# Mixer tiles loaded into copy pages, a column sum's adding transfer in two halves and one gain held back, in a one-core encoder kernel

## The chip, the core and the metric

The kernel runs on one core of a Trainium2 chip. A core has TensorE (PE, the matrix engine), VectorE (DVE), ScalarE (ACT), GpSimd (POOL) and SyncE (SP), each with its own queue of instructions that it works off in order. SP issues most transfers (DMAs); POOL issues those that add to what lies at their destination. Sixteen DMA engines move the data. The metric is the time of one execution on the device in microseconds (us), as the median of three runs.

## What is computed

The reference is one layer of an encoder trunk on x of 1024 positions by 1024 channels, in float32:

```
proj = rmsnorm(x) @ w_in                    # 1024 x 8192, cut into glu_in, q, v, z_f, z_b, og, g_a, g_b
a    = silu(layernorm(dwconv31(glu(glu_in)))) @ conv_pw_w
o    = scan_forward(q, v, z_f) + scan_backward(q, v, z_b)      # 8 heads of 128, gated linear recurrence
bmix = (o * rsqrt(mean(o*o) + eps) * norm_w * silu(og)) @ hgrn_o_w
x    = x + (sigmoid(g_a) * a + sigmoid(g_b) * bmix) @ w_out
gate, val = split(rmsnorm(x) @ ffn_w_up)    # 2 x 2816 columns
x    = x + (silu(dwconv3(gate)) * val) @ ffn_w_down
out  = rmsnorm(x) * final_norm_w
```

## The kernel before

**Layout and products.** Activations stand transposed, 128 channels on the partitions and a half of 512 positions along them, in tiles of 128 x 512. Each float32 operand is split into a high and a low part (`split`, line 124: ACT casts the high part, DVE subtracts it from the source for the low part), and `mm3` (lines 148 to 150) makes a product of three matmuls: high by high, high by low, low by high. Split activations live in 32 pages `hx`, weights in four pages `wp` and three `wq`; raw weights come into two pages `wr`, other tiles into four pages `tm` (`tmp`, filled by `load`, line 117) and three pages `ev`.

**Pairs.** `pair_job` computes two column tiles of a projection at once with seven products in place of eight, from sums of the four weight quadrants. `rows` is the first tile's weights, `col` holds the column sums in a page `sw`: line 374 loads the first halves of both tiles into `col` and line 375 the second, then the whole second tile is added onto it by one transfer (`add`, line 301, issued by POOL; 512 KB). `sums` then makes row sums in place with two more adding transfers: `rows[:, :nk]` takes `col[:, nk:]`, and `rows[:, nk:]` takes `rows[:, :nk]`. They may begin when the split of `rows` into products 1 and 2 has read it. Products run in the order 1, 2, 6, 7, 5, 4, 3; 6 and 3 use the row sums, 7 and 5 the column sums. This form serves 13 of 19 pairs of the input projection (the other six add on DVE) and 19 of 22 pairs of the FFN (the other three load sums stored earlier).

**The scan.** While dense products run, 16 items (8 heads by 2 halves) go through the scan. `scan_base` and `scan_levels` use eight pages `A` of the pool `hp` for interleaved copies (`woven`, line 1177); the last matmuls that read them are on line 1196. `scan_states` transposes the keys, copies them to `kT` on ACT (line 1326) and copies the backward states to `Sb` (lines 1351 and 1353). `outputs` then sweeps `Sb` on DVE (line 1431), multiplies on PE (line 1374), takes means of squares, scales on ACT (line 1393), transposes, multiplies by gain and gate on DVE (line 1402) and stores the mixer tile in `d_bm` (line 1406). Head 7 is split at once instead.

**The seam.** After the last head, `bm_loads(half)` loads the seven stored tiles of a half through `load` into `tm` pages and splits them into `hx`, first half 0, later half 1. Around it run the pointwise convolution, whose results `gated_a` multiplies by a gate from `d_ga` and stores in `d_a` (lines 1104 to 1106), then the product with `hgrn_o_w`, whose results `merge` (lines 1511 to 1513) multiplies by a gate from `d_gb` and adds to `d_a`. `weight_sums` loads FFN weights (line 1544) beside it.

**The end.** The last four FFN rows are added in three parts: half 0, then two quarters of half 1, for each of eight column tiles. Per tile `final_evac` adds on DVE (line 1889), `turn_out` transposes back (line 1900), squares and sums on ACT (line 1902) and multiplies by the final gain on DVE (line 1915); after the eighth tile come the reduction, the power on POOL (line 1912), the scaling (lines 1936 and 1938) and the store (line 1940).

**What sets the order.** PE's order is that of the program. The order on the other engines, and on SP's queue, is chosen when the kernel is built, by a planner that goes by priority in program order and by estimated times; `pin` (`keep_in_program_order`) fixes instructions among themselves, and `tc.issue_after(i)` puts all instructions of a block that are on `i`'s engine behind `i`.

Of the kernel before, what the change touches and what calls it, by code (L numbers as in the profile page):

```python
# [15 lines left out]
ALU = mybir.AluOpType  # L16
AX = mybir.AxisListType

P = 128
# [18 lines left out]
def view(t, off, dims):  # L38

    return bass.AP(  # L40
        tensor=t.tensor,
        offset=t.offset + off,
        ap=[list(t.ap[0])] + [list(d) for d in dims],
    )
# [3 lines left out]
def tile_hybrid_encoder(  # L48
# [22 lines left out]
    nc = tc.nc  # L71
    PSUM = bass.MemoryType.PSUM
    V, A, G, T = nc.vector, nc.scalar, nc.gpsimd, nc.tensor

    S, D = x.shape[1], x.shape[2]
    ND = D // P
# [6 lines left out]
    NH = D // DK  # L83
# [19 lines left out]
    def page(pool, tag, bufs, dt=F32):  # L103
        return pool.tile([P, H], dt, tag=tag, name=nm(tag), bufs=bufs)
# [7 lines left out]
    def hx():  # L112
        return page(mp, "hx", 32, F32R)

    def load(src):
        t = tmp()
        nc.sync.dma_start(t, src)
        return t


    pin = tc.keep_in_program_order

    def split(hi, lo, src, eng, late=False):
        parts = A.copy(hi, src), eng.tensor_tensor(lo, src, hi.bitcast(F32), op=ALU.subtract)  # L124
        if late:
            for i in parts:
                pin(i)
        return hi, lo
# [153 lines left out]
    def pair_job(src0, src1, nk, acts, wpool, pool, evac, su=4, first=False, late=False, now=False, direct=False, columns=1, take=None, stored=None):  # L282
# [7 lines left out]
        def steps(w):  # L290
# [4 lines left out]
            def add(o, a):  # L295
                if first:
                    V.tensor_tensor(o, o, a, op=ALU.add)
                elif direct:
                    pin(V.tensor_tensor(o, o, a, op=ALU.add))
                else:  # L300
                    G.dma_start(o, a, accum_op=ALU.add)

            if take is not None:
# [11 lines left out]
                if stored is None:  # L315
# [3 lines left out]
                    col, sums, a22 = raw(), rows, other[:, nk:]  # L319
# [23 lines left out]
            def column_page():  # L343
                return wpool.tile([P, 2 * nk, P], F32, tag="sw", name=nm("sw"), bufs=columns)
# [26 lines left out]
                return  # L371

            col = column_page()
            nc.sync.dma_start(col[:, :nk], src0[:, :nk])
            nc.sync.dma_start(col[:, nk:], src1[:, :nk])
            if first:
                other = column_page()
                nc.sync.dma_start(other, src1)
                add(col, other)
            elif not direct:  # L380
                add(col, src1)
            def sums():
                add(rows[:, :nk], col[:, nk:])
                add(rows[:, nk:], rows[:, :nk])
# [757 lines left out]
    def tt(o, a, b, op=ALU.mult):  # L1142
        return V.tensor_tensor(o, a, b, op=op)  # L1143

    last_keys = []

    kscale = cp.tile([P, 2 * NH], F32, name="kscale")
    V.tensor_scalar(kscale, lbw[:, 3, :], DK**-0.5, None, op0=ALU.mult)
# [168 lines left out]
    def scan_states(i, kG, v, Tt, Sf, Sb):  # L1317

        half = i % 2
        kTs = []  # L1320
        for d in range(2):
            b = bank("mm" if d else "tr")
            for c in range(4):
                T.transpose(b[:, c * P : (c + 1) * P], kG[:, d, c * P : (c + 1) * P], ident)
            kT = page(hp, "kT", 2)
            A.copy(kT, b)
            kTs.append(kT)
        yield
        for d in range(2):
            u = bank("mm" if d else "sc")  # L1330
            for c in range(4):
                sl = slice(c * P, (c + 1) * P)
                T.matmul(u[:, sl], kTs[d][:, sl], v[:, c, :], start=True, stop=True)
            u4 = c4(u)
            if d == 0:
                for c in range(4 if half == 0 else 3):
                    nx = Sf[half][:, c + 1, :] if c < 3 else Sf[1][:, 0, :]
                    if half == 0 and c == 0:
                        V.tensor_copy(nx, u4[:, 0, :])
                    else:  # L1340
                        V.scalar_tensor_tensor(
                            nx,
                            Sf[half][:, c, :],
                            Tt[:, half, 0, c : c + 1],
                            u4[:, c, :],
                            op0=ALU.mult,
                            op1=ALU.add,
                        )
            else:

                A.copy(Sb[half][:, 0:3, :], u4[:, 1:4, :])
                if half == 1:
                    A.copy(Sb[0][:, 3, :], u4[:, 0, :])
        yield

    def scan_outputs(h, kept, Sf, Sb):


        ons, gates = [], []
        ss = cp.tile([P, 2, 4], F32, name=nm("oss"), tag="oss", bufs=2)  # L1360
        rs = cp.tile([P, 2, 4], F32, name=nm("ors"), tag="ors", bufs=2)
        for half in range(2):
            S_t, v, qF = kept[half]
            o = bank("ob")
            for c in range(4):
                sl = slice(c * P, (c + 1) * P)
                g = half * 4 + c
                terms = [(S_t[:, c, :], v[:, c, :])]
                if g > 0:
                    terms.append((qF[:, 1, sl], Sf[half][:, c, :]))  # L1370
                if g < 7:
                    terms.append((qF[:, 0, sl], Sb[half][:, c, :]))
                for n, (l, r) in enumerate(terms):
                    T.matmul(o[:, sl], l, r, start=(n == 0), stop=(n == len(terms) - 1))
            on = tmp()
            A.copy(on, o)
            for c in range(4):
                junk = hp.tile([P, DK], F32, tag="jk", name=nm("jk"), bufs=1)
                A.activation(  # L1379
                    junk, on[:, c * P : (c + 1) * P], AF.Square, accum_out=ss[:, half, c : c + 1]  # L1380
                )
            ons.append(on)
            gates.append(page(hp, "og", 2))
            nc.sync.dma_start(gates[half], d_og[h][half])
            if half == 0:
                yield
        rstd_small(rs, ss, DK)
        yield
        yield
        for half in range(2):  # L1390
            for c in range(4):
                sl = slice(c * P, (c + 1) * P)
                A.activation(
                    ons[half][:, sl], ons[half][:, sl], AF.Copy, scale=rs[:, half, c : c + 1]
                )
            yield
        for half in range(2):
            b = bank("tr")
            for c in range(4):
                T.transpose(b[:, c * P : (c + 1) * P], ons[half][:, c * P : (c + 1) * P], ident)  # L1400
            bt = ev()
            V.scalar_tensor_tensor(bt, b, vec("hn", h), gates[half], op0=ALU.mult, op1=ALU.mult)
            if h == NH - 1:
                bm[h][half] = split(hx(), hx(), bt, V)
            else:
                nc.sync.dma_start(d_bm[h][half], bt)
            yield
# [35 lines left out]

    def bm_loads(half):
        for h in range(NH - 1):
            bm[h][half] = split(hx(), hx(), load(d_bm[h][half]), V)

    NI = 2 * NH
    cur = Base(scan_inputs(0))
# [433 lines left out]

    PARTS = [(0, range(4)), (1, range(2)), (1, range(2, 4))]
    y_tags = itertools.cycle(["tr", "sc"])

    def final_evac(i, half, chunks, acc):
        t = xr[i][half][:, chunks[0] * P : (chunks[-1] + 1) * P]
        V.tensor_tensor(t, acc, t, op=ALU.add)
        later(8 - len(chunks), lambda: turn_out(i, half, chunks))  # L1890

    def turn_out(i, half, chunks):

        t, n = xr[i][half], len(chunks)
        if i == 0 and chunks[0] == 0:
            out_y.append(fy.tile([P, 4, D], F32, tag="y", name=nm("y"), bufs=2))
        ss, y = out_ss[half], out_y[half]
        b = bank(next(y_tags))[:, : n * P]
        for m, c in enumerate(chunks):
            T.transpose(b[:, m * P : (m + 1) * P], t[:, c * P : (c + 1) * P], ident)  # L1900
        for m, c in enumerate(chunks):
            A.activation(
                out_junk[c % 2], b[:, m * P : (m + 1) * P], AF.Square, accum_out=ss[:, i, c : c + 1]
            )
        those = slice(chunks[0], chunks[-1] + 1)
        if i == ND - 1:
            rs = cp.tile([P, 4], F32, name=nm("frs"), tag="frs", bufs=2)[:, :n]
            V.tensor_reduce(
                rs, ss[:, :, those].rearrange("p i c -> p c i"), axis=AX.X, op=ALU.add
            )  # L1910
            V.tensor_scalar(rs, rs, 1.0 / D, EPS, op0=ALU.mult, op1=ALU.add)
            G.tensor_tensor(rs, rs, mhalf.to_broadcast([P, n]), op=ALU.pow)
            for m, c in enumerate(chunks):
                out_r[half, c] = rs[:, m : m + 1]
        gain = V.tensor_tensor(
            y[:, those, i * P : (i + 1) * P],
            b.rearrange("p (c e) -> p c e", e=P),
            view(fnw, i * P, [[0, n], [1, P]]),
            op=ALU.mult,
        )  # L1920
        if i == ND - 1:
            pin(gain)

    def finish(half, chunks, late=2):
        for n, c in enumerate(chunks):
# [124 lines left out]
```

## Time and profile before

| | us |
|---|---|
| median of three runs | 1725.66 |
| lowest, highest | 1725.45, 1726.85 |
| the profiled execution | 1724.33 |
| its span, first to last instruction | 1722.5 |

The lines of the profile name the engine, the line of the kernel, the operation and its tiles (output, then inputs). `x12` is a count; a bracket tells how long the engine was idle ahead of the row, and what ended that. "SPq" is SP's issue of a transfer, "PEld" a load of weights into PE. A wait for several things is put down to the one that came last by the profile, so a row can name the wrong one. Times are those of one execution; the stage of a time can be told by its lines.

### The profile page before, as it was taken

The page shows a single profiled execution, that of the slowest core. Times are in us where ns is not written, and L with a number is a line of the kernel's source. Part 1 is how long each engine was busy: PE and PEld are TensorE (multiplying, and loading weights), DVE is VectorE, ACT ScalarE, POOL GpSimd, SP SyncE. Part 2 cuts the span into 40 slices and gives each one's busy share as a digit, 9 for nine tenths or more (in the row PEclk, how much of TensorE's full clock was granted, in tenths as well). Part 3 has the DMA queues.
Part 4 walks back from the last instruction along what each step waited for, and adds up shares of the span by engine and source line. Part 5 has one row for each costly group of instructions (what it writes and reads, how often), then busy time and mean ns, then how long its engine had stood idle before and what let it go on. Part 6 is the DMA issues. An engine that isn't in the chain of part 4 may idle for free. (4 is left out here: it accounts for less than half of the span.)

```text
span 1722.5 us, 30765 instructions
## 1 busy us (share of the span) xinstructions
PE 1698.2 (99%) x11902; PEld 1414.3 (82%) x11902; DVE 1255.7 (73%) x1937; ACT 826.1 (48%) x1544; POOL 207.6 (12%) x249
## 2 busy tenths in 40 slices
PE   8999999999999999999999999999999999999997
PEld 6878888788788888888878888888888888888777
DVE  4599999745778888888556466667767776657864
ACT  7444443334566777776442245444334434542334
POOL 2211111100001111111100002011111111000110
PEclk9999999999999999999999999999999999999999
DMA  8778888854673434436579466577777876783842
GB/s 288 240 171 185 197 194 192 199 165 146 207 246 100 137 127 133 127 116 208 182 259 324 147 206 198 147 156 158 160 169 168 174 175 154 237 261 104 211 92 99
DMA packets 336586, 308.29 MB, mean 179 GB/s; under 512 B 17071, under 2 KB 248631, under 8 KB 336439
## 3 DMA queue, kind: packets, MB, share of 16 engines
q1 hardware_dynamic: 289590, 267.51, 48.9%
q0 software_dynamic: 46848, 38.81, 15.5%
q8 instruction: 93, 1.52, 0.3%
q14 instruction: 55, 0.44, 0.1%
HBM read 201.40 MB, written 87.03 MB: 167 GB/s over the span
## 5 line engine op out<-in xcount | busy, mean ns | idle before, releaser
L148 PE MATMUL mm<-hx,wp 128*128 128x512 f32 x1068 | 427.0, 400 | 3.0 <-ACT tm L850 1.5
L150 PE MATMUL mm<-hx,wp 128*128 128x512 f32 x1068 | 417.1, 390 | 0.8 <-DVE wp L124 0.8
L149 PE MATMUL mm<-hx,wp 128*128 128x512 f32 x1068 | 416.3, 390 | 1.2 <-DVE hx L124 1.2
L124 ACT CAST wp<-wr 128x1024 fp32r<-128x1024 f32 (+2 forms) x147 | 147.2, 1002 | 246.3 <-PE mm L149 130.2
L148 PEld LDWEIGHTS mm<-hx,wp 128*128 128x128 f32 x1068 | 200.6, 188 | 45.8 <-DVE ev L799 2.3
L150 PEld LDWEIGHTS mm<-hx,wp 128*128 128x128 f32 x1068 | 200.5, 188 | 45.3 <-DVE wp L124 2.5
L149 PEld LDWEIGHTS mm<-hx,wp 128*128 128x128 f32 x1068 | 200.8, 188 | 40.8 <-DVE hx L124 1.6
L124 DVE TENSOR_TENSOR wp<-wr,wp 128x1024 fp32r<-128x1024 f32 (+2 forms) x145 | 169.1, 1167 | 64.0 <-ACT wp L124 61.6
L1038 DVE SCALAR_TENSOR_TENSOR acc<-gl,v_b,acc 128x1024 f32<-128x1024 f32 x120 | 148.6, 1271 | 0.4
L439 ACT COPY su<-mm 128x512 f32<-128x512 f32 x82 | 47.6, 581 | 62.2 <-PE mm L150 62.0
L1143 DVE TENSOR_TENSOR qF<-qF,tb 128x512 f32<-128x512 f32 x96 | 65.6, 684 | 13.6 <-ACT A L1177 13.0
L1314 POOL DMA_DIRECT2D S<-D x64 | 36.2, 572 | 284.9 <-ACT jk L1379 129.5
L124 ACT CAST wq<-sw 128x1024 fp32r<-128x1024 f32 x41 | 43.2, 1053 | 57.0 <-PE mm L149 41.8
L148 PE MATMUL tr<-hx,wp 128*128 128x512 f32 x180 | 70.5, 392 | 0.0
L150 PE MATMUL tr<-hx,wp 128*128 128x512 f32 x180 | 70.1, 389 | 0.0
L149 PE MATMUL tr<-hx,wp 128*128 128x512 f32 x180 | 70.0, 389 | 0.0
L1646 DVE SCALAR_TENSOR_TENSOR tm<-gp,v_a,tm 128x512 f32<-128x512 f32 x88 | 65.9, 749 | 3.9 <-ACT tm L1644 2.0
L1143 DVE TENSOR_TENSOR kG<-kG,tb 128x512 f32<-128x512 f32 x96 | 65.5, 685 | 4.4 <-ACT A L1177 2.5
L148 PE MATMUL mm<-hy,wp 128*128 128x512 f32 x164 | 64.2, 391 | 0.0
L148 PE MATMUL sc<-hy,wq 128*128 128x512 f32 x164 | 64.2, 391 | 0.0
L150 PE MATMUL sc<-hy,wq 128*128 128x512 f32 x164 | 63.8, 389 | 0.0
L149 PE MATMUL mm<-hy,wp 128*128 128x512 f32 x164 | 63.8, 389 | 0.0
(373 smaller groups left out, 3673.9 us busy)
## 6 DMA issues: line engine op xcount, KB each, us to landing
wr<-in_w_in_dram SPq DMA_DIRECT2D x48, 512.0 KB, 4.4
wr<-in_ffn_w_up_dram SPq DMA_DIRECT2D x22, 512.0 KB, 3.9
sw<-in_w_in_dram SPq DMA_DIRECT2D x38, 256.0 KB
d_g<-ft SPq DMA_DIRECT2D x38, 256.0 KB, 3.2
sw<-in_ffn_w_up_dram SPq DMA_DIRECT2D x38, 256.0 KB, 3.6
sw<-in_ffn_w_up_dram POOLq DMA_DIRECT2D x19, 512.0 KB, 8.0
wr<-sw POOLq DMA_DIRECT2D x32, 256.0 KB, 3.5
wr<-wr POOLq DMA_DIRECT2D x32, 256.0 KB, 3.7
```

The source lines that it names most:

```text
L124: parts = A.copy(hi, src), eng.tensor_tensor(lo, src, hi.bitcast(F32), op=ALU.subtract)
L148: T.matmul(acc, whi[:, k, :], ahi, start=first, stop=False, skip_group_check=again)
L149: T.matmul(acc, whi[:, k, :], alo, start=False, stop=False, skip_group_check=again)
L150: T.matmul(acc, wlo[:, k, :], ahi, start=False, stop=last, skip_group_check=again)
L439: A.copy(t, acc)
L1038: V.scalar_tensor_tensor(acc, g[:, k : k + S], tap(k), acc, op0=ALU.mult, op1=ALU.add)
L1143: return V.tensor_tensor(o, a, b, op=op)
L1314: G.dma_start(S_t[g : g + 32, :, g : g + 32], D_t[g : g + 32])
L1646: V.scalar_tensor_tensor(c, g[:, o + k : o + k + H], vec("fdw", k * NF + j), c, op0=ALU.mult, op1=ALU.add,)
```

## The change

1. In `pair_job`, the load of `col`'s second half (from the second tile) is issued ahead of that of the first, and the adding transfer of the whole page becomes two of 256 KB, second half first. `col[:, nk:]` is what the row sums read.
2. `bm_loads` loads into pages `A` of the scan in place of `tm`. The splits of heads 0 to 5 are put behind the last copy to `kT` on ACT (`last_turned`, line 1326), that of head 6 behind the last scaling (`last_scaled`, line 1393).
3. At the end, the multiplication by the gain for tile 5 of the last quarter (`i == ND - 3`) is kept and issued behind the last addition of line 1889, that of tile 7.

```diff
--- before.py
+++ after.py
@@ -371,14 +371,15 @@
                 return
 
             col = column_page()
+            nc.sync.dma_start(col[:, nk:], src1[:, :nk])
             nc.sync.dma_start(col[:, :nk], src0[:, :nk])
-            nc.sync.dma_start(col[:, nk:], src1[:, :nk])
             if first:
                 other = column_page()
                 nc.sync.dma_start(other, src1)
                 add(col, other)
             elif not direct:
-                add(col, src1)
+                for part in (slice(nk, 2 * nk), slice(nk)):
+                    add(col[:, part], src1[:, part])
             def sums():
                 add(rows[:, :nk], col[:, nk:])
                 add(rows[:, nk:], rows[:, :nk])
@@ -1142,7 +1143,7 @@
     def tt(o, a, b, op=ALU.mult):
         return V.tensor_tensor(o, a, b, op=op)
 
-    last_keys = []
+    last_keys, last_turned, last_scaled = [], [], []
 
     kscale = cp.tile([P, 2 * NH], F32, name="kscale")
     V.tensor_scalar(kscale, lbw[:, 3, :], DK**-0.5, None, op0=ALU.mult)
@@ -1323,7 +1324,7 @@
             for c in range(4):
                 T.transpose(b[:, c * P : (c + 1) * P], kG[:, d, c * P : (c + 1) * P], ident)
             kT = page(hp, "kT", 2)
-            A.copy(kT, b)
+            last_turned[:] = [A.copy(kT, b)]
             kTs.append(kT)
         yield
         for d in range(2):
@@ -1390,9 +1391,10 @@
         for half in range(2):
             for c in range(4):
                 sl = slice(c * P, (c + 1) * P)
-                A.activation(
+                done = A.activation(
                     ons[half][:, sl], ons[half][:, sl], AF.Copy, scale=rs[:, half, c : c + 1]
                 )
+            last_scaled[:] = [done]
             yield
         for half in range(2):
             b = bank("tr")
@@ -1443,7 +1445,11 @@
 
     def bm_loads(half):
         for h in range(NH - 1):
-            bm[h][half] = split(hx(), hx(), load(d_bm[h][half]), V)
+            t = page(hp, "A", 8)
+            nc.sync.dma_start(t, d_bm[h][half])
+            behind = last_turned if h < NH - 2 else last_scaled
+            with tc.issue_after(behind[0].ins):
+                bm[h][half] = split(hx(), hx(), t, V)
 
     NI = 2 * NH
     cur = Base(scan_inputs(0))
@@ -1883,10 +1889,16 @@
 
     PARTS = [(0, range(4)), (1, range(2)), (1, range(2, 4))]
     y_tags = itertools.cycle(["tr", "sc"])
+    gains = []
 
     def final_evac(i, half, chunks, acc):
         t = xr[i][half][:, chunks[0] * P : (chunks[-1] + 1) * P]
-        V.tensor_tensor(t, acc, t, op=ALU.add)
+        added = V.tensor_tensor(t, acc, t, op=ALU.add)
+        if i == ND - 1 and chunks[-1] == 3 and half:
+            with tc.issue_after(added.ins):
+                for gain in gains:
+                    gain()
+            gains.clear()
         later(8 - len(chunks), lambda: turn_out(i, half, chunks))
 
     def turn_out(i, half, chunks):
@@ -1912,14 +1924,21 @@
             G.tensor_tensor(rs, rs, mhalf.to_broadcast([P, n]), op=ALU.pow)
             for m, c in enumerate(chunks):
                 out_r[half, c] = rs[:, m : m + 1]
-        gain = V.tensor_tensor(
-            y[:, those, i * P : (i + 1) * P],
-            b.rearrange("p (c e) -> p c e", e=P),
-            view(fnw, i * P, [[0, n], [1, P]]),
-            op=ALU.mult,
-        )
-        if i == ND - 1:
-            pin(gain)
+
+        def gain():
+            return V.tensor_tensor(
+                y[:, those, i * P : (i + 1) * P],
+                b.rearrange("p (c e) -> p c e", e=P),
+                view(fnw, i * P, [[0, n], [1, P]]),
+                op=ALU.mult,
+            )
+
+        if i == ND - 3 and half and chunks[-1] == 3:
+            gains.append(gain)
+        elif i == ND - 1:
+            pin(gain())
+        else:
+            gain()
 
     def finish(half, chunks, late=2):
         for n, c in enumerate(chunks):
```

## What was expected, before the result

> **What bounds the kernel now.** First the page's shares of busy time.
>
> ```profile
> span 1722.5 us, 30765 instructions
> PE 1698.2 (99%) x11902; PEld 1414.3 (82%) x11902; DVE 1255.7 (73%) x1937; ACT 826.1 (48%) x1544; POOL 207.6 (12%) x249
> ```
>
> TensorE (PE) is busy in all but 1722.5 - 1698.2 = 24.3 us. So an edit can win only from these 24.3 us, and what it does to other engines counts where PE comes to wait. Where the idle time lies is in the windows; columns are stretch, its length, then busy time of PE, its weight loads, VectorE (DVE), ScalarE (ACT) and GpSimd (POOL), clock, DMA share, GB/s.
>
> ```profile
> 100.00:200.00 100.00, 100.00 (x442) 82.52 (x441) 100.00 (x120) 43.41 (x61) 16.34 (x18) 1.00 0.77 179
> 850.00:880.00 30.00, 30.00 (x166) 25.42 (x164) 12.51 (x24) 12.58 (x37) 1.86 (x2) 1.00 0.71 230
> 880.00:900.00 20.00, 18.11 (x79) 14.29 (x78) 14.17 (x21) 8.98 (x15) 0.00 (x0) 1.00 0.88 277
> 900.00:960.00 60.00, 60.00 (x267) 49.67 (x266) 39.38 (x57) 14.17 (x19) 0.00 (x0) 1.00 0.90 286
> 1300.00:1400.00 100.00, 100.00 (x443) 82.81 (x442) 76.55 (x103) 41.28 (x58) 17.59 (x16) 1.00 0.78 178
> ```
>
> The adding transfers run in the pairs of the input projection and of the FFN; the first and the last row are stretches of these, and PE is busy all the time there, at full clock, a matmul every 100/443 = 0.226 us (one lasts 0.39 us in the rows, so they overlap, and I argue from PE's waits, not from its share). The mixer loads sit at the seam between the pointwise convolution and the `hgrn_o_w` product, 860 to 900 us: 20.00 - 18.11 = 1.89 us idle. The held gains sit at the very end. PE's list of waits (total, times, longest) has two more beside the pairs:
>
> ```profile
> PE mm L148 <- DVE ev L799: 1.0, 1, 1.0
> PE mm L148 <- ACT su L439: 0.9, 1, 0.9
> ```
>
> **Mixer loads in copy pages, the term that counts.** The timelines of PE, DVE, SP and ACT at the seam (start, duration, engine, line, and in brackets the idle time before it with its releaser):
>
> ```profile
> 880.49 0.47 PE L148 MATMUL mm<-hx,wp 128*128 128x512 f32 x1 [0.35 <-ACT hx L124]
> 881.53 0.50 PE L150 MATMUL mm<-hx,wp 128*128 128x512 f32 x1 [0.34 <-DVE wp L124]
> 896.85 0.39 PE L148 MATMUL mm<-hx,wp 128*128 128x512 f32 x1
> 898.44 0.50 PE L149 MATMUL mm<-hx,wp 128*128 128x512 f32 x1 [1.20 <-DVE hx L124]
> 897.10 0.69 DVE L1512 TENSOR_TENSOR ev<-mm,ev 128x512 f32<-128x512 f32 x1 [1.09 <-PE mm L150]
> 897.70 0.68 DVE L124 TENSOR_TENSOR hx<-ev,hx 128x512 fp32r<-128x512 f32 x1
> 889.55 2.77 SPq L117 DMA_DIRECT2D tm<-d_bm  x3
> 878.33 0.62 ACT L124 CAST hx<-tm 128x512 fp32r<-128x512 f32 x1 [2.02 <-DMA tm<-d_bm]
> 878.85 1.05 ACT L124 CAST wp<-wr 128x1024 fp32r<-128x1024 f32 x1
> ```
>
> The 1.20 us: PE wants the low half of the last mixer page, whose subtraction (897.70) stands on DVE behind the merge product (897.10, line 1512). That row blames PE, but PE had ended that sum two sums earlier (24 matmuls each); what it lacked was the gate page. SP had stood from 889.55 us in three mixer loads, each waiting for one of the four `tm` pages, and sent for the gate behind them. The chain of waits and SP's own list:
>
> ```profile
> 892.37 4.61 DMA ev<-d_gb
> SPq L117 <- DVE hx L124: 6.0, 6, 1.4
> ```
>
> The gate lands at 892.37 + 4.61 = 896.98 us, just ahead of 897.10. The 0.35 and 0.34 us have the same root: ACT stood 2.02 us for a mixer load (878.33), and the cast of the weights that PE then lacked (878.85) stood behind it.
>
> The change takes eight `A` pages for the 14 loads. Their last readers, and what the split is now tied to:
>
> ```profile
> L1196 PE MATMUL ob<-A,A x64: 196/196/217, 836.3 to 836.9; 128*32 128x32 f32 x64
> L1406 SPq DMA_DIRECT2D d_bm<-ev x14: 319/319/691, 584.3 to 848.9; - x14
> L117 SPq DMA_DIRECT2D tm<-d_bm x14: 319/345/441, 861.7 to 892.0; - x14
> 849.04 0.59 ACT L1326 COPY kT<-mm 128x512 f32<-128x512 f32 x1
> 852.17 0.48 ACT L1351 COPY Sb<-mm 128x384 f32<-128x384 f32 x1 [1.40 <-PE mm L1333]
> L124 ACT CAST hx<-tm x14: 603/621/627, 871.2 to 894.7; 128x512 fp32r<-128x512 f32 x14
> ```
>
> All eight pages are free at 837 us. Two stores per head in steps of (848.9 - 584.3)/6 = 44 us leave heads 0 to 5 stored by 805 us, so the first loads may leave SP from 837 us on instead of 861.7 us, and the later ones as casts free pages; only head 6 must wait. The casts come behind the last `kT` copy (849.6 us), for head 6 behind the last scaling (line 1393). Six casts of the first half at 0.62 us are 3.7 us of ACT, the subtractions as much of DVE (0.68 us each); both engines are idle for over 17 of the 30 us from 850 to 880 us. The second half can be cast only when the convolution pages of `hx` are read, close to 881 us, but its data is then there, and the product wants it from 892 us. What SP is moved past are the gate loads, `d_a` stores and weight loads of 840 to 892 us: 14 issues of 0.35 us, without the waits. The sum: idle 0.35 + 0.34 + 1.20 = 1.89 us, and, as each stall also costs the overlap of 0.39 - 0.226 = 0.16 us, **2.4 us** if all three go; the bounds are 2.4 and, below nothing, the third rival's price. I take 2.4: from 900 to 1590 us PE's list has no wait, so what is won at the seam is kept, and the cover that could fail is DMA, 0.90 busy from 900 to 960 us, whose work comes earlier here and does not grow.
>
> The edge adds a wait: behind the first casts on ACT stand the weight casts and, at 852.17, the `Sb` copies. For these:
>
> ```profile
> 855.53 0.34 DVE L1431 SCALAR_TENSOR_TENSOR Sb<-Sb,Tt 128x128 f32<-128x128 f32 x1
> 857.46 0.39 PE L1374 MATMUL ob<-v,S 128*128 128x128 f32 x2
> ```
>
> The sweep that starts from `Sb` ends at 855.87 us, and PE wants it at 857.46 us: 1.6 us of cover.
>
> **The adding transfer in halves, and the swapped loads.** Rows from the transfers' group, the page's DMA issues (KB each, us from issue to landing) and the waits of 1100 to 1470 us:
>
> ```profile
> L301 POOL DMA_DIRECT2D wr<-sw x32: 857/893/919, 124.6 to 1452.9; - x32
> L301 POOL DMA_DIRECT2D sw<-in_ffn_w_up_dram x19: 1580/1580/1665, 1099.7 to 1443.9; - x19
> sw<-in_ffn_w_up_dram POOLq DMA_DIRECT2D x19, 512.0 KB, 8.0
> wr<-sw POOLq DMA_DIRECT2D x32, 256.0 KB, 3.5
> ACT wp L124 <- DMA wr<-wr: 75.3, 12, 7.6
> ```
>
> 32 pairs (13 and 19) each get two issues of about 0.89 us for one of 1.58 us, 0.2 us more on an engine that is 12% busy. The half that the row sums read should land after some 4 us instead of 8.0 us, though the row sum's own packets may queue behind the second half, which leaves perhaps 1 to 4 us. Is that on the path? In 12 FFN pairs the cast of the row sums waits for their landing, so it is late, but PE does not wait. The latest one:
>
> ```profile
> 1368.29 1.05 ACT L124 CAST wp<-wr 128x1024 fp32r<-128x1024 f32 x1 [7.62 <-DMA wr<-wr]
> 1369.37 1.22 DVE L124 TENSOR_TENSOR wp<-wr,wp 128x1024 fp32r<-128x1024 f32 x1 [3.44 <-ACT wp L124]
> 1370.93 0.39 PE L150 MATMUL mm<-hx,wp 128*128 128x512 f32 x1
> ```
>
> The low part is ready at 1370.59 us, and PE reads it at 1370.93 us: 0.34 us to spare. So the gain is **nothing**: PE's own products cover the lateness, and the edit only widens a narrow margin. If instead the row sums came later, say by the 0.9 us of one more issue, the latest pair would stall PE for 0.9 - 0.34 = 0.56 us. The 12 waits have a mean of 75.3/12 = 6.3 us against 7.6 for this one, so the usual late pair has 1.3 us more to spare and wouldn't stall: about 1 us in all. The bounds are 1 us lost and, as PE waits for no row sum, nothing won; I take 0. The swap of two loads of 0.4 us each on SP goes with it at nothing.
>
> [...]
>
> **The held gain at the end.** The last DVE and PE rows:
>
> ```profile
> 1713.36 0.42 DVE L1915 TENSOR_TENSOR y<-sc,fnw 128x256 f32<-128x256 f32 x1 [0.90 <-ACT oj L1902]
> 1713.70 0.41 DVE L1889 TENSOR_TENSOR xr<-mm,xr 128x256 f32<-128x256 f32 x1
> 1713.03 0.28 PE L150 MATMUL mm<-hx,gx 128*128 128x256 f32 x1
> 1714.26 0.41 PE L1900 MATMUL sc<-ident,xr 128*128 128x128 f32 x2 [0.73 <-ACT oj L1902]
> ```
>
> PE ends the last sum at 1713.31 us; its addition (1713.70) waits behind the gain of 1713.36 us; the last transposes follow 0.15 us after it (the row names ACT, but the addition ends last that they need). Put behind, the gain lets the addition start about 0.3 us earlier; squares, power, scaling and store follow as before. The gain itself (0.42 us on DVE) then lies beside the last transposes and ACT's squares, so nothing is lost. **0.3 us**, bounds 0 and 1713.70 - 1713.36 = 0.34.
>
> **The sum.** The profiled execution took 1724.33 us (span 1722.5 and 1.8 around it): 1724.33 - 2.4 - 0 - 0.3 = 1721.6. The median is 1725.66, 1.3 above it, so the forecast is 1725.66 - 2.7 = **1723.0 us**.
>
> **Rivals.** *A new wait takes the seam's place* (0.20): another instruction in the queues holds the merge product or a weight cast, or the pages don't come free as I think. For it: `hx`, not `tm`, may be what is short, as the second half's pages free only near 881 us, and `ev` has three pages. Against: SP's list names the page waits, 6.0 us. It leaves the end's gain alone: 1725.66 - 0.3 = 1725.3 us.
>
> *More goes than I count* (0.20): earlier row sums shift the order of other work on DVE and ACT, and the two lone stalls inside the pairs go (1.0 + 0.9 us, with the overlap 2.2): 1723.0 - 2.2 = 1720.8 us. For it: the first lies where the convolution's taps fill DVE (the first window row). Against: neither row names a transfer.
>
> *The casts block ACT* (0.10), the slower side: placed ahead of the `Sb` copies, they wait there for loads that SP sends too late. A late landing of 4.6 us as the gate's and 3.7 us of casts, less the cover of 1.6 us, is 6.7 us of PE's time ahead of line 1374; 1723.0 + 6.7 = 1729.7 us. It decides once the casts ahead of `Sb` end after 853.8 us (852.17 + 1.6). Against: pages free at 837 us leave 12 us until the last `kT` copy ends, for loads of some 4 us.
>
> **Chances.** Forecast 0.50, rivals 0.20, 0.20, 0.10. A measurement here tells about 0.2% from no change, 3.45 us: 1722.2 and 1729.1 are the bounds. Faster: the second rival and a little of the forecast, 0.22; slower: the third, 0.10; within: 0.68. The range 1720.2 to 1727.0 holds the forecast and the first two rivals with the unknown 1 us of the halves on top, and leaves out the third and the edges.
>
> **What would show it.** Right: mixer loads leave SP from about 840 us, no PE idle between 880 and 900 us, pairs without PE waits, the last addition ahead of a gain at line 1915. Fewer casts of line 124 wait for `wr<-wr`. Wrong: PE waits before line 1374 near 857 us, or on `hx` near 897 us still, or inside the FFN pairs.

## The result and the profile after

| | before | changed |
|---|---|---|
| median of 13 runs each, side by side | 1725.45 | 1721.84 |
| lowest, highest | 1722.95, 1730.1 | 1720.41, 1723.85 |
| the profiled execution | 1724.33 | 1721.94 |
| its span | 1722.5 | 1720.0 |

The ratio is 0.9978, interval 0.997 to 0.9986: 3.6 us less, where 2.7 were forecast, barely more than a measurement tells from no change. In three later comparisons before ran at 1729.0 to 1730.3 us, and the changed kernel, in two of them, at 1722.9 and 1723.0, which is some 6 us. So the changed kernel varies less than before does, and how much it wins depends on how badly before does. That was not foreseen, and most experiments below turn on it.

In the listing after, lines 382 to 1393 stand 1 later than before, and those behind by more: line 1374 is 1375, 1393 is 1394, 1431 is 1433, 1511 and 1512 are 1517 and 1518, 1889 is 1896, 1900 is 1912, 1915 is 1929, and the mixer loads moved from line 117 to 1449. First the page's busy time, then the windows (stretch, length, busy time of PE, its loads, DVE, ACT, POOL, then clock, DMA share, GB/s):

```profile
span 1720.0 us, 30762 instructions
...
PE 1699.1 (99%) x11902; PEld 1416.2 (82%) x11902; DVE 1256.6 (73%) x1937; ACT 825.0 (48%) x1544; POOL 240.7 (14%) x281
```

```profile
850.00:880.00 30.00, 29.76 (x162) 25.12 (x161) 15.97 (x31) 16.51 (x45) 1.86 (x2) 1.00 0.87 291
880.00:900.00 20.00, 20.00 (x92) 16.56 (x91) 14.34 (x22) 5.62 (x9) 0.00 (x0) 1.00 0.84 267
900.00:960.00 60.00, 60.00 (x266) 49.71 (x265) 36.21 (x50) 13.80 (x19) 0.00 (x0) 1.00 0.78 237
```

PE is no longer idle from 880 to 900 us, where it lost 1.89 us. In exchange 0.24 us of idle time are new between 850 and 880 us. The DMA work moved forward: its share rises from 0.71 to 0.87 ahead of 880 us, and falls from 0.90 to 0.78 behind 900 us.

The mixer loads, by group (ns least, median, most; first and last start), and the timeline of DVE and SP around the gate:

```profile
L1449 SPq DMA_DIRECT2D A<-d_bm x14: 319/422/1142, 827.5 to 864.7; - x14
```

```profile
886.83 0.68 DVE L124 TENSOR_TENSOR hx<-ev,hx 128x512 fp32r<-128x512 f32 x1
887.06 0.32 SPq L1517 DMA_DIRECT2D ev<-d_gb  x1
...
889.90 0.69 DVE L1518 TENSOR_TENSOR ev<-mm,ev 128x512 f32<-128x512 f32 x1 [2.39 <-DMA ev<-d_gb]
```

The last mixer load leaves SP at 864.7 us, before at 892.0 us. The gate load is issued at 887.06 us with no mixer load ahead of it, and the low half of the last mixer tile is made at 886.83 us; before, at 897.70 us, PE stood waiting for it.

The new wait, on PE and DVE behind 855 us:

```profile
855.11 0.34 DVE L1433 SCALAR_TENSOR_TENSOR Sb<-Sb,Tt 128x128 f32<-128x128 f32 x1
855.37 0.68 DVE L124 TENSOR_TENSOR hx<-A,hx 128x512 fp32r<-128x512 f32 x1
855.98 0.34 DVE L1433 SCALAR_TENSOR_TENSOR Sb<-Sb,Tt,Sb 128x128 f32<-128x128 f32 x1
...
857.96 0.68 DVE L124 TENSOR_TENSOR hx<-A,hx 128x512 fp32r<-128x512 f32 x1
...
858.57 0.33 DVE L1433 SCALAR_TENSOR_TENSOR Sb<-Sb,Tt 128x128 f32<-128x128 f32 x1
...
858.96 0.49 PE L1375 MATMUL ob<-Sb,qF 128*128 128x128 f32 x2 [0.24 <-DVE Sb L1433]
```

Six steps of the sweep, each waiting for the one before, now alternate on DVE with subtractions for the early mixer tiles and with products of `gated_a`. The last step ends at 858.57 + 0.33 = 858.90 us, against 855.87 us before.

The end, and the FFN pairs (waits of 1097 to 1480 us: total, times, longest; then the group of the halved additions; then their landing):

```profile
1710.86 0.28 PE L150 MATMUL mm<-hx,gx 128*128 128x256 f32 x1
...
1711.18 0.42 DVE L1896 TENSOR_TENSOR xr<-mm,xr 128x256 f32<-128x256 f32 x1 [0.89 <-PE mm L150]
...
1711.52 0.41 DVE L1929 TENSOR_TENSOR y<-sc,fnw 128x256 f32<-128x256 f32 x1
...
1711.75 0.41 PE L1912 MATMUL sc<-ident,xr 128*128 128x128 f32 x2 [0.39 <-DVE xr L1896]
```

```profile
POOL wr L301 <- DVE wp L124: 127.3, 19, 7.5
ACT wp L124 <- PE mm L149: 88.5, 21, 4.4
```

```profile
L301 POOL DMA_DIRECT2D sw<-in_ffn_w_up_dram x38: 1288/1303/1892, 1097.8 to 1441.5; - x38
```

```profile
sw<-in_ffn_w_up_dram POOLq DMA_DIRECT2D x38, 256.0 KB, 6.2
```

The addition now stands ahead of the gain: the last transposes follow the last sum by 1711.75 - 1710.86 = 0.89 us, before by 1714.26 - 1713.03 = 1.23 us. In all 19 FFN pairs the row sums start when DVE has read `rows`, and no cast waits for their landing any more (12 did). An addition of 256 KB takes POOL 1.3 to 1.9 us to issue, not the 0.89 us priced, and lands in 6.2 us, not in about 4.

### The profile page after: what moved, and what is told of

It is laid out like the page before. It is cut to its first block, busy times and chain, and to the rows that moved or that the text cites. A ratio compares the mean times of both kernels' runs of the same rounds, so it can differ in the third digit from the quotient of the medians.

```text
span 1720.0 us, 30762 instructions
## 1 busy us (share of the span) xinstructions
PE 1699.1 (99%) x11902; PEld 1416.2 (82%) x11902; DVE 1256.6 (73%) x1937; ACT 825.0 (48%) x1544; POOL 240.7 (14%) x281
## 4 chain that ended last, share of the span: by engine, by line
PE 61%; DVE 1%; ACT 1%; DMA 0%; issue 0%; POOLq 0%; ACTq 0%; SPq 0%; DVEq 0%
PE mm L148 14%; PE mm L150 14%; PE mm L149 14%; PE sc L148 3%; PE sc L150 3%; PE sc L149 3%; PE ob L1375 2%; PE tr L148 1%; PE tr L150 1%; PE tr L149 1%; PE sc L1197 1%; PE sc L1283 1%; PE mm L1334 1%; PE sc L1334 1%; PE ob L1197 0%
## 5 line engine op out<-in xcount | busy, mean ns | idle before, releaser
L301 POOL DMA_DIRECT2D sw<-in_ffn_w_up_dram x38 | 49.8, 1498 | 116.5 <-DMA sw<-in_ffn_w_up_dram 76.7
L148 PE MATMUL mm<-hy,wp 128*128 128x512 f32 x164 | 64.2, 391 | 0.0
```

The source lines that it names most:

```text
L148: T.matmul(acc, whi[:, k, :], ahi, start=first, stop=False, skip_group_check=again)
```

## The experiments

**Reading two traces against each other.** PE runs the same 11902 matmul instructions in the same order in every kernel here, but for six neighbours at 838 us in those with pages. So the start of the k-th one can be set against that of the k-th one in the profiled execution of before, and the lag at the end of each stage tells where time was lost (+) or won (-). The stages are in before's time: 872 to 920 us holds the seam's three stalls, 920 to 1600 us the FFN pairs, "end" is behind 1705 us.

| run | to 120 | to 840 | to 872 | to 920 | to 1600 | to 1705 | end | sum |
|---|---|---|---|---|---|---|---|---|
| before again (b0) | 2.26 | 0.66 | 0.00 | 1.08 | 0.31 | -0.16 | -0.01 | 4.14 |
| e3, gain only | 2.00 | 0.35 | 0.00 | 0.52 | 3.78 | 0.01 | -0.34 | 6.32 |
| e1, pages only | 0.48 | 0.27 | 0.51 | -2.70 | 0.62 | -0.11 | 0.01 | -0.92 |
| e2, halves only | 0.25 | 1.06 | 0.00 | 0.09 | -0.03 | 1.08 | 0.00 | 2.45 |
| e4, without pages | -0.26 | -1.00 | 0.00 | 0.29 | -0.01 | 0.18 | -0.32 | -1.12 |
| changed | 1.06 | -0.20 | 0.52 | -2.69 | -0.01 | -0.87 | -0.32 | -2.51 |
| changed again (a0) | -0.20 | 0.42 | 1.19 | -2.70 | -0.01 | 0.73 | -0.35 | -0.92 |
| changed again (a1) | 0.25 | 0.22 | 1.03 | -2.11 | -0.04 | -0.46 | -0.34 | -1.45 |
| e10, no swap | 0.23 | -0.57 | 0.82 | -2.70 | -0.01 | -0.15 | -0.32 | -2.70 |
| e7, halves reversed | -0.27 | 1.67 | 0.91 | -2.38 | -0.02 | 0.59 | -0.34 | 0.16 |
| e9, behind the sweep | 0.00 | -0.35 | 0.00 | -2.71 | 0.00 | 0.98 | -0.34 | -2.42 |
| e5, no edge | 0.57 | 5.05 | -0.01 | -1.84 | -0.04 | 0.42 | -0.34 | 3.81 |
| e8, added twice | 0.92 | 6.07 | 1.14 | -2.69 | 14.62 | 0.15 | -0.35 | 19.86 |

The columns "to 840" and "to 1705" move by up to a microsecond or more with no edit to explain it. So can the others: the changed kernel's 1.06 us "to 120" arise ahead of 60 us, before any halved addition, and b0 loses 1.08 us more than before in the seam's own stalls. The others are read below with that in mind.

### Each part alone

Each of e1 to e3 is before with one of the three edits as the diff has it; e4 is the changed kernel with the loads back in `tm`, the order edges kept:

```diff
-            t = page(hp, "A", 8)
-            nc.sync.dma_start(t, d_bm[h][half])
+            t = load(d_bm[h][half])
```

> The kernel before with the mixer loads in copy pages and their two edges alone. The page theory (the seam's stalls came from loads that waited for tm pages on SP, and nothing else of the change touches PE) expects no PE idle time from 880 to 900 us, where it was 1.89, at most 0.3 us new before line 1374, and 2 to 2.6 us less in all: about 1723.2 against 1725.5. The order theory (the gain came mainly from earlier row sums in the pairs) expects the seam to win 1 us at most, about 1724.5.

> The kernel before with the swapped loads and the adding transfer in two halves alone. The page theory expects the time of before within 1 us (1724.5 to 1726.5), PE waits of before at the seam, and yet no cast of line 124 in the FFN pairs that waits for wr<-wr, where 12 did. The order theory expects at least 1 us less, with the two lone stalls inside the pairs gone.

> The kernel before with the held gain alone. Both theories expect 0.3 us less, which the times cannot tell from nothing; the profile can: from the start of the last matmul of line 150 to the start of the last transposes it was 1.23 us (1713.03 to 1714.26), and it should be 0.9.

> The changed kernel with the mixer loads back in tm pages, the edges, halves and held gain kept. The page theory expects the seam's stalls back: 1 to 2 us of PE idle from 880 to 900 us, SP waiting in line 117 for its pages, and a time 1.5 to 2.5 us over the changed kernel. If the edges made the gain and not the pages, the seam stays free of idle time and the time stays that of the changed kernel.

| | median (lowest, highest) | ratio to before (interval) |
|---|---|---|
| before | 1730.32 (1725.64, 1737.8) | |
| e1, pages only | 1728.69 (1723.7, 1732.71) | 0.9989 (0.9974 to 1.0004) |
| e2, halves only | 1725.28 (1723.95, 1728.18) | 0.9968 (0.9957 to 0.998) |
| e3, gain only | 1730.3 (1726.95, 1732.99) | 0.9997 (0.9984 to 1.0011) |
| e4, without pages | 1724.09 (1722.15, 1726.44) | 0.9963 (0.995 to 0.9975) |

The halves, to which the forecast gave nothing, win 5.0 us here by the medians, and most of the spread goes with them. They do so without the order theory's route: the two lone stalls are still in e2, at 1.1 and 1.0 us. Pages alone and the gain alone can't be told from before by time. So the theory that the pages bring the time, some 2.7 us whatever the chip, fell for the time, though not for the stalls: by the trace pages and gain do what was forecast. With pages PE is not idle from 880 to 900 us; with the order edges but without pages (e4) it is, so the pages do it. The window of e1, then that of e4:

```profile
880.00:900.00 20.00, 20.00 (x92) 16.57 (x91) 15.34 (x23) 5.95 (x9) 0.00 (x0) 1.00 0.93 284
```

```profile
880.00:900.00 20.00, 18.84 (x79) 14.70 (x80) 13.79 (x22) 9.07 (x14) 0.00 (x0) 1.00 0.91 287
```

Where whole transfers lose time is shown by e3, whose additions are those of before. Its waits in 1100 to 1500 us, and a piece of its timeline:

```profile
ACT wp L124 <- DMA wr<-wr: 115.1, 17, 8.8
```

```profile
1162.96 1.05 ACT L124 CAST wp<-wr 128x1024 fp32r<-128x1024 f32 x1 [8.60 <-DMA wr<-wr]
1163.91 0.58 ACT L439 COPY su<-mm 128x512 f32<-128x512 f32 x1
...
1164.54 0.50 PE L148 MATMUL mm<-hx,wp 128*128 128x512 f32 x1 [0.34 <-ACT su L439]
```

17 casts come late, and PE stands now, but its row names a copy of line 439: the copy that frees an accumulator stands on ACT behind the late cast. From 1140 to 1190 us e3 falls behind by 2.8 us, and by 3.8 us over the FFN pairs. The same pairs cost 0.62 us in e1, 0.31 us in b0 and nothing in the profiled execution of before. In every kernel with halves, nine profiles besides e8, they cost the same to within 0.04 us.

The theory formed from this is called the margin theory below: late row sums are free up to a margin, the whole transfer passes it in some executions, and the halves keep within it. Its rivals are that what counts is something narrower in the edit (which half goes first, or the earlier start by the swapped loads), and the forecast's reading, by which PE's own products cover late row sums.

### Which half goes first, and whether the swap matters

In e7 the halves are added in the other order; in e10 the two loads have their old order:

```diff
-                for part in (slice(nk, 2 * nk), slice(nk)):
+                for part in (slice(nk), slice(nk, 2 * nk)):
```

```diff
-            nc.sync.dma_start(col[:, nk:], src1[:, :nk])
             nc.sync.dma_start(col[:, :nk], src0[:, :nk])
+            nc.sync.dma_start(col[:, nk:], src1[:, :nk])
```

> The changed kernel once more, beside the others of this chip. The margin theory (the row sums of the pairs run so close to PE's need that in some executions, and on some chips in most, PE stalls; the halves take that away, the pages the seam's stalls, the held gain 0.3 us) expects the gain to be as large as this chip's transfers are late: 3 to 8 us, and runs that spread half as far as those of before. The page theory of the prediction expects 2.7 us on every chip.

> The changed kernel with the two adding transfers in the other order, the half that the row sums don't read first. Same work, same order otherwise. The margin theory expects the row sums as late as in the kernel before or 0.5 us later: ten or more FFN casts that wait for wr<-wr, and the time 1 to 5 us over the changed kernel, by the chip. If two shorter transfers make the gain and not which one goes first, the time is that of the changed kernel within 1 us.

> The changed kernel with the two loads of the column sums back in their old order (first half, then second), so that the half that is added first is loaded last and no addition can start before both loads are nearly there. Early start theory (what halving wins is that an addition begins once its own half is loaded): part of the lateness comes back, at least 6 of the 19 casts of row sums in the FFN pairs wait for wr<-wr again, and the time is 1 to 3 us above that of the changed kernel of the same call. Two short transfers theory (what is won is that a half lands sooner after its issue than the whole did, 6 us against 8 to 9): at most 3 such casts wait, and the time is within 0.7 us of the changed kernel.

> The changed kernel, to stand beside the others of this call: 1722 to 1723.5 us, at most 3 casts of the FFN pairs wait for wr<-wr, and no PE wait of over 0.5 us in these pairs.

e7 takes 1722.25 us (1721.71 to 1724.6), ratio 0.9959 (0.9945 to 0.9973), beside the changed kernel's (a0) 1722.92 us (1721.78 to 1723.59), ratio 0.9959 (0.9945 to 0.9973). e10 takes 1722.77 us (1721.64 to 1723.57), ratio 0.9967 (0.9954 to 0.9979), beside 1722.98 us (a1, 1721.24 to 1723.78), ratio 0.9967 (0.9955 to 0.998). In the FFN waits of e7, then of e10:

```profile
POOL wr L301 <- DVE wp L124: 126.4, 19, 7.3
...
ACT wp L124 <- DMA wr<-wr: 4.4, 1, 4.4
```

```profile
ACT wp L124 <- DMA wr<-wr: 31.6, 6, 6.2
```

So "the half that the row sums use sent first" is not what helps: sent last, one cast waits, as in the changed kernel measured beside it, where the margin theory expected ten or more and 1 to 5 us lost. Loaded last, six casts wait, as the early start theory has it, but no time is lost, as the theory of two short transfers has it. The split into two is what matters; the order of the loads adds margin that these runs did not need.

### The price of late row sums

In e8 the second half is added twice. Its column sums, and what follows from them, are others.

```diff
-                for part in (slice(nk, 2 * nk), slice(nk)):
+                for part in (slice(nk, 2 * nk), slice(nk, 2 * nk), slice(nk)):
```

> The changed kernel with the half that the row sums use added twice, so its column sums, and what is computed from them, are others: one more transfer of 256 KB on POOL's queue in 32 pairs, ahead of the row sums. Margin theory (PE stalls once row sums come more than some 4 us later than in the changed kernel, 1361.9 us to land against about 1366 us at which the cast must start): row sums some 4 to 6 us later, at least 15 casts of the FFN pairs wait for wr<-wr, PE waits for su copies or the row sums' low parts in the pairs, and 3 to 40 us more than the changed kernel. The forecast's reading (PE's own products cover late row sums): many casts wait, but PE does not, and the time stays within 2 us.

> The kernel before once more, for its waits on a chip of this set. Margin theory: if its time is above 1727 us, its FFN pairs hold PE waits of 0.3 to 2 us behind late casts of row sums (wr<-wr), which the profiled execution of 1724.33 us did not have; at a time near 1725 us they are absent. The forecast's reading: no PE wait in the pairs whatever the time, and any excess lies elsewhere.

e8 takes 1748.44 us (1744.18 and 1752.69), ratio 1.0116 (1.0087 to 1.0144), 25 us more than the changed kernel. Its waits of 1097 to 1480 us:

```profile
ACT wp L124 <- DMA wr<-wr: 145.0, 18, 9.8
...
PE mm L148 <- ACT su L440: 7.2, 7, 2.5
```

Once row sums are late enough, PE stands: over the FFN pairs at the copies of `su`, as in e3, 14.6 us by the lag; in the input projection some 6 us, mostly behind DVE's line 800 (5.5 us in six waits). So the reading that PE's products cover late row sums holds only within a margin, and one transfer more is past it.

b0 was one execution of 1728.46 us, near the median of 1729.31 of before beside it. The margin theory expected waits of 0.3 to 2 us in its FFN pairs. They cost it 0.31 us, with 15 late casts, so the theory accounts for little of its 4.1 us:

```profile
ACT wp L124 <- DMA wr<-wr: 94.2, 15, 8.1
```

Over half, 2.26 us, was lost before 120 us. The windows there of b0, of the profiled execution of before, and of the changed one:

```profile
90.00:95.00 5.00, 5.00 (x23) 4.13 (x22) 5.00 (x8) 2.62 (x4) 0.00 (x0) 1.00 1.22 267
95.00:100.00 5.00, 2.81 (x11) 1.97 (x10) 3.00 (x5) 2.54 (x4) 0.00 (x0) 0.91 0.82 270
100.00:105.00 5.00, 5.00 (x18) 3.98 (x17) 5.00 (x9) 1.56 (x4) 0.74 (x5) 0.75 0.34 108
```

```profile
95.00:100.00 5.00, 3.46 (x15) 2.74 (x15) 4.74 (x7) 2.80 (x5) 0.15 (x1) 1.00 0.82 261
100.00:105.00 5.00, 5.00 (x22) 3.86 (x21) 5.00 (x8) 2.15 (x3) 0.59 (x4) 1.00 0.44 139
```

```profile
95.00:100.00 5.00, 3.55 (x16) 2.61 (x15) 5.00 (x7) 2.92 (x5) 0.00 (x0) 1.00 0.61 180
100.00:105.00 5.00, 5.00 (x23) 3.93 (x22) 5.00 (x9) 2.65 (x4) 0.75 (x5) 1.00 0.62 219
```

PE waits once at about 97 us for ACT to empty an accumulator (line 850), in b0 for 2.19 us, and its granted clock in the two stretches is 0.91 and 0.75. This wait is 1.5, 2.0, 2.0 and 2.2 us in the four profiles with whole additions (before, e1, e3, b0) and 1.4 to 1.7 us in the nine with halves. The first pair's addition of the input projection is issued at 85 us, just ahead of it, and ACT's weight cast ahead of the wait stood 2.1 us in b0 for its load, against 0.3 us in the profiled execution of before. That the shorter additions let those loads land sooner fits these rows; no run took this addition alone, so the link is argued, not shown.

### The edge that keeps the early splits back, and one more

In e5 the splits are free to go as soon as their data is there; e9 puts them behind the last step of the sweep as well, so that DVE's subtractions can't stand between its steps.

```diff
-            behind = last_turned if h < NH - 2 else last_scaled
-            with tc.issue_after(behind[0].ins):
-                bm[h][half] = split(hx(), hx(), t, V)
+            bm[h][half] = split(hx(), hx(), t, V)
```

```diff
-            V.scalar_tensor_tensor(
+            swept = V.scalar_tensor_tensor(
                 Sb[hf][:, cc, :],
...
+        last_swept[:] = [swept]
...
-            with tc.issue_after(behind[0].ins):
+            with tc.issue_after(behind[0].ins), tc.issue_after(last_swept[0].ins):
```

> The changed kernel without the two edges, so that the planner may put the casts of the mixer tiles on ACT where it likes. If the edges guard PE (the rival that the casts block ACT), casts come ahead of the copies to kT or the scaling, and PE waits 1 to 5 us more between 836 and 872 us. If they don't matter, the waits there stay at 0.24 us and the time within 1 us of the changed kernel.

> The changed kernel with the subtractions of the mixer tiles put behind the last step of the sweep on DVE as well. The changed kernel shows a new wait of 0.24 us for that sweep, whose six steps alternate there with subtractions. Expected: the sweep ends 1 to 3 us earlier, the 0.24 us go, nothing comes in their place from 860 to 900 us, and the time is 0 to 0.5 us under the changed kernel, less than the times can tell.

e5 takes 1728.33 us (1725.18 to 1729.96), ratio 0.9992 (0.9983 to 1.0001): without the edge nearly all of the gain is gone. Its waits and its window:

```profile
ACT hx L124 <- DMA A<-d_bm: 5.5, 2, 3.9
...
PE sc L1334 <- ACT kT L1327: 2.9, 1, 2.9
```

```profile
820.00:840.00 20.00, 17.09 (x239) 15.45 (x238) 12.74 (x28) 11.23 (x34) 3.58 (x6) 0.91 0.63 198
```

Casts stand on ACT for loads that have not landed, with the `kT` copies behind them, and PE stands for those: 2.9 us, and a clock of 0.91 behind it, 4.6 us in the lag between 800 and 840 us. This is the third rival, which the edge keeps out.

e9 takes 1721.79 us (1721.46 to 1722.48), ratio 0.9954 (0.994 to 0.9968), 1.1 us below the changed kernel beside it (a0), though the intervals overlap. Its windows:

```profile
850.00:880.00 30.00, 30.00 (x166) 25.54 (x166) 18.19 (x33) 16.21 (x43) 1.85 (x2) 1.00 0.89 290
880.00:900.00 20.00, 20.00 (x90) 16.55 (x89) 16.04 (x23) 5.80 (x10) 0.00 (x0) 1.00 0.97 295
```

No stall is left at the seam: the 0.5 to 1.2 us that the other kernels with pages and the first edge lose up to 872 us are 0.00 here. That is shown by the trace; the times can't tell e9 from the changed kernel.

## Why the prediction held, and where it did not

**The median came near the forecast in part by luck.** In the two profiled executions seam and gain win 2.2 + 0.3 = 2.5 us net, close to the 2.7 forecast, and the other stages cancel. But what a comparison measures holds the halves too, priced at nothing: where before ran at 1729.0 and 1729.3 us, the same change won 6 us, more than twice the forecast.

**The seam (2.4 us) was right in mechanism.** In the changed profile all three stalls went, the loads left SP from 827.5 us, the gate is no longer queued behind them. Gross it was more, 2.7 us in most profiles (2.1 in a1, where 0.30 us of idle time stayed at 882 us): the three idle times of 0.35, 0.34 and 1.20 us cost 0.6, 0.6 and 1.5 us of lag. The forecast added 0.16 us of lost overlap to each, taking the usual 0.39 us for the first matmul behind a wait; its own rows show 0.47 to 0.50 us, and 0.50 - 0.226 = 0.27 us is what they cost. These stalls differ between executions too: the other four profiles that load into `tm` lose 0.09 to 1.08 us more there than the one that was read.

**A wait came in its place, by another road than the rival's.** "Both engines are idle for over 17 of the 30 us" hid that DVE's subtractions would fall between steps of a chain that PE wants 1.6 us later. The cover was reckoned against ACT's casts, and DVE used it up: 0.5 to 1.2 us lost, so the seam's net is 1.1 to 2.2 us in the profiles with pages and both edges as in the diff. e9 shows the cause by removing it.

**The held gain (0.3 us) was right:** 0.32 to 0.35 us in each kernel that has it, 0.01 us or less in those without.

**The halves (0 us, "nothing won") were mis-sized, and this is the term that failed.** "PE's own products cover the lateness, and the edit only widens a narrow margin" was true of the execution that was read, and the late pairs with 0.34 us to spare were in its rows. What was wrong was the bound: a margin of 0.34 us under a landing time that differs from one execution to the next (12, 15 and 17 late casts in the profiles of before, b0 and e3, the longest waits 7.6, 8.1 and 8.8 us) is itself a loss, in some of them. The four profiles with whole additions lose 0, 0.31, 0.62 and 3.78 us in the FFN pairs, a mean of 1.2 us, and the nine with halves nothing. By time the halves alone are worth 5.0 us on the chip of e2. The profiles give 1.2 us for the FFN pairs and, if the start belongs to the halves, a mean lag there of 1.2 us without them less 0.2 us with them, 1.0 us more. Two things on record bear on the rest of the 5.0 us. The four profiles are no fair sample: e1's is the fastest of its twelve executions, while e3's, at 1730.65 us, lies at the median of its own, and there start and FFN pairs lose 2.00 + 3.78 = 5.8 us, 1.7 of them through the clock (last section). And as far as means tell, the halves do not save drops of the clock: recorded with each time, it is 0.9983 on average over the 35 executions of before and over the 11 of e2 alike, where a difference of 0.001 would be 1.7 us. So the late row sums are the likeliest place, but one profile stands for some ten runs, and the split of the 5.0 us stays open.

So the margin theory holds for its direction (e3, e8) and not for its whole size (b0). The details of the step were off as well: POOL spends 33 us more, not 6, which nothing waited for; the halves land in 6.2 us, not in some 4, and the rows beside that figure show two different transfers, 8.0 us for 512 KB from HBM and 3.5 us for 256 KB within SBUF; and which half comes first doesn't matter.

**The rivals.** *More goes than I count* comes as near in time (1720.8 against 1721.84 us measured) as the forecast does, but not by its route: the two lone stalls are still there, 0.7 and 0.8 us. *A new wait* came true in part. *The casts block ACT* is real, 4.6 us without the edge against 6.7 reckoned, at the copies to `kT` (line 1334 waits) rather than at line 1375; the edge keeps it out.

## What to carry to other kernels

A late arrival that costs nothing in one trace is priced by its spare time, not by its wait: where transfers land late in 12 of 19 rounds and the latest has 0.3 us to spare, other executions can stall, as e3's did, and a cut in the lateness is worth most on those. Two executions of the same program, laid against each other matmul by matmul, show in which stage they differ and which differences an edit never touches. Work moved forward into idle time must be placed behind the chains there on every engine that it uses: on ACT the edge saved some 5 us, on DVE a second one the 0.5 to 1.2 us of its wait in the traces.

## What the runs showed of the hardware

**In four profiles a PE wait of 2 to 3 us cost some 1.7 us more through the clock.** After PE waits of 1.98 us (e3), 2.19 us (b0), 2.52 us (e8) and 2.91 us (e5) the granted clock fell. The windows of e3, of e8 and of e5; those of b0 stand above:

```profile
95.00:100.00 5.00, 3.02 (x11) 2.17 (x10) 3.19 (x5) 2.65 (x4) 0.06 (x1) 0.85 0.88 284
100.00:105.00 5.00, 5.00 (x20) 3.99 (x19) 5.00 (x8) 1.71 (x3) 0.69 (x5) 0.81 0.33 114
```

```profile
1285.00:1290.00 5.00, 2.76 (x7) 1.93 (x8) 3.27 (x5) 2.77 (x4) 1.94 (x3) 0.81 1.12 226
1290.00:1295.00 5.00, 5.00 (x20) 3.98 (x20) 4.87 (x7) 2.79 (x5) 0.93 (x1) 0.85 1.24 276
```

```profile
835.00:840.00 5.00, 4.22 (x21) 4.05 (x22) 3.12 (x7) 3.92 (x14) 1.41 (x2) 0.66 0.40 141
```

Summed over its stretches, each fall lacks 0.34 of 5 us, which is 1.7 us of PE's time. From 100 to 105 us PE ran 18 matmuls in b0 and 20 in e3, against 22 in the profiled execution of before. After a wait of 2.0 us in e1 and after all of 1.7 us or less at that place (about 97 us) it stayed at 1.00, so the length of the wait alone doesn't decide; what does is open. In b0 the wait was 0.65 us longer than in the profiled execution of before and the lag grew by 2.0 us. In e5 the recorded clock of the twelve executions is 0.9973 on average, against 0.9983 for the changed kernel beside it, which fits one such drop in most of them.

**Two additions of 256 KB from HBM are not half of one of 512 KB.** In the FFN pairs they land in 6.2 us (changed) against 8.0 us (before), and take 1.29 to 1.89 us each to issue against 1.58 us and more, while additions of 256 KB within SBUF (`wr<-sw`) take 0.86 to 0.90 us in the changed kernel and land in 3.3 us. In before the five issues of `wr<-sw` from 100 to 200 us, where DVE is 100% busy, took 884 to 898 ns, and all 32 took 857 to 919 ns.
